# Layer 0's last grouped head, reordered at its end, and sixteen modulation loads moved to GpSimd's queue

## The chip, the cores and the metric

One NeuronCore of a Trainium2 chip runs the whole kernel. It has five engines with a queue of instructions each: TensorE (PE in the profile, with its weight loads as PEld), VectorE (DVE), ScalarE (ACT), GpSimd (POOL) and SyncE (SP), which here only issues transfers (DMAs). The metric is the device time of one execution in microseconds (us); lower is better.

## The reference

Two layers of a diffusion backbone work on 512 latent and 256 context tokens of width 1024, all in float32.

```python
hx = _rmsnorm(x, norm_g) * (1.0 + scale_x) + shift_x        # the same for the context: hc
a_att = _na_latent(qa, ka, va, cka, cva, rpb, rows)          # 8 heads, neighbourhood window plus all context keys
b_att = _gqa_latent(qb, k_all, v_all)                        # 8 query heads, 2 key heads, all 768 keys
o_a = (a_att * jax.nn.silu(a_z)) @ w_o_a
o_b = (b_att * jax.nn.silu(b_z)) @ w_o_b
merged = jax.nn.sigmoid(g_a) * o_a + jax.nn.sigmoid(g_b) * o_b
x_new = x + gate_x * (merged @ w_out)
```

`shift`, `scale` and `gate` are the modulation: `silu(c) @ w_ada + b_ada`, a vector times a 1024x3072 matrix for each layer, once for the latent and once for the context condition. In layer 0 the context tokens go through the same steps, except that they attend only to context keys (`c_a_att`, `c_b_att`). Layer 1 updates the latent tokens alone.

## The kernel before

**Precision.** Every matrix product of activations and weights is three matmuls on high and low parts (`mm3`, lines 352 to 354): high x high, high x low, low x high. So each operand has to be split: ScalarE copies the high part (`S.copy`, which rounds), and VectorE or GpSimd subtracts it from the source for the low part. Weights are split so in `load_w` (lines 322 and 325) and `load_w2` (337 and 339), where even tiles' low parts go to GpSimd and odd ones' to VectorE (`mix_lo`).

**Stages of a layer.** The projections come first, then neighbourhood attention by head, the grouped projections, grouped attention by head, and a merge: the branch's output projections (`o_chunks`, "a" as filler during grouped attention, "b" after it), and the output projection `w_out` with the residual. While a head's softmax runs, PE gets pieces of projections from a list, `fill`.

**A grouped head.** `gq_scores` (line 948) makes four score tiles of 768 columns in a score bank (`s`, two buffers of 1024 columns) and their softmax; `ctx_scores` (725) makes the context queries' scores. `gq_values` (964) transposes the probabilities in six steps of four blocks (670), splits them (673 on ACT, 674 on DVE) and multiplies by the values (973, 974) into the one value bank (`v`). `ctx_values` (741) does the same for the context's 256 columns (747, 748), also in the `v` bank. Each ends in `head_out` (677): ACT copies one half of the result (682), DVE adds the other (683), and GpSimd multiplies it into the gate path `zb` (684), 64 rows by 512 or 256 columns. `values_of` (866) calls the main values first, then the context's.

**After the last head.** `zb` has four blocks f of 768 columns; head h writes block h // 2. `hilo` (555) splits a block: ACT the high part `gbh` (558), GpSimd the low part `gbl` (559). `early` (985) splits blocks 0 to 2 before head 7's values are traced, and line 1003 splits block 3 after them. Then `o_chunks("b", ...)` takes four chunks of 256 output channels; a chunk has four pieces, for two f each of (0, 512) and (512, 768) columns, and a piece sums over the four blocks of `zb`. Its results lie in the `f` bank and five `x` banks that take the place of the score and value banks (`open_ps(x=5)`, line 997).

**The modulation of layer 1** is computed in layer 0. `ada_steps` (239) loads tiles of 128x512 from `w_ada` (251, buffer `rawb`, two of them) and multiplies each twice by the broadcast condition `cb` in one VectorE instruction with a running sum (258). The first 16 tiles come early in layer 0; the second 16 (line 1031) run in the merge, some after each of the six token tiles of `w_out`. `make_hx` (291) then builds layer 1's normalised input from each token tile, with the row norm on GpSimd (286, 288); the latent tiles are also stored to DRAM (1047), from where layer 1's merge reads them back.

**What sets the order.** The kernel is traced in program order, and a planner with a model of each instruction's cost lays every engine's queue out from it: among the instructions that are ready by its clock, it takes the earliest traced. A few chains are tied to program order by hand (`behind`, line 381, for the dot products on VectorE). Each queue then runs strictly in that order on the chip, so an instruction that waits holds everything behind it.

Of the kernel before, what the change touches and what calls it, by code (L numbers as in the profile page):

```python
# [12 lines left out]
ALU = mybir.AluOpType  # L13
# [55 lines left out]
def hybrid_kernel(es: ExitStack, tc, x, ctx, cvec, w_ada, w_ada0, small, gvec, w_in, w_o_a, w_o_b, w_out,  # L69
# [168 lines left out]

    def ada_steps(l, tiles, halves, nv, pool):

        cb = {}

        def load(h):
            cb[h] = pool.tile([128, 2, 512], F32, tag="cb", name=nm("cb"), bufs=1)
            for v in range(nv):
                src = cd[8 * v + 4 * h:8 * v + 4 * h + 4].rearrange("k p -> (k p)").unsqueeze(0)
                nc.sync.dma_start(cb[h][:, v, :], src.to_broadcast([128, 512]))

        def load_tile(h, i):
            cb["w"] = pool.tile([128, 512], F32, tag="rawb", name=nm("rawb"), bufs=2)  # L250
            nc.sync.dma_start(cb["w"], w_ada[l, h, i])

        def dot(h, i, v):
            if v == 0:
                load_tile(h, i)
            w = cb["w"]
            o = w if v == nv - 1 else pool.tile([128, 512], BF16, tag="junk", name=nm("junk"), bufs=1)
            behind(ON_DVE, lambda: V.tensor_tensor_reduce(o, w, cb[h][:, v, :], 1.0, 0.0, ALU.mult, ALU.add,
                                                          asum[:, i, h, v:v + 1]))
# [231 lines left out]
    def layer(l, hx, nxt, mid):  # L491
# [62 lines left out]

        def hilo(src, dst, fs):
            sv = src.rearrange("p (f n) -> p f n", f=4)
            for f in fs:
                S.copy(R(dst[0][:, f, :ntok]), sv[:, f, :ntok])
                G.tensor_tensor(R(dst[1][:, f, :ntok]), sv[:, f, :ntok], dst[0][:, f, :ntok], ALU.subtract)

# [3 lines left out]
        def o_chunks(br, prepare, evac):  # L564

            src = (w_o_a if br == "a" else w_o_b)[l]
            act = lambda part, k: gated[br][part][:, k, :]
            res = []
            for i in range(4):
                st = {}  # L570

                def ld(i=i, st=st):
                    st["w"] = load_w2(src, 256 * i, 4, mix_lo)
                pieces = [lambda f=f, n0=n0, n1=n1, i=i, st=st:
                          chan_proj(st["w"], f, act, n0, n1, lambda f, a, b, ps: evac(2 * i + f, a, b, ps))
                          for f in range(2) for n0, n1 in spans]
                res.append((ld, ([prepare] if i == 0 and prepare else []) + pieces))
            return res
# [72 lines left out]
        if True:  # L651
# [25 lines left out]
            def head_out(po, e, dst):  # L677
# [5 lines left out]
                V.tensor_tensor(t1[m:m + 64, :n], po[m:m + 64, :n], t1[m:m + 64, :n], ALU.add)  # L683
                G.tensor_tensor(dst, dst, t1[m:m + 64, :n], ALU.mult)

# [55 lines left out]
            def ctx_values(p, vsl, dst, e):  # L741
                hi, lo = transpose_split(
                    [(p[:, 256 * i + 128 * k:256 * i + 128 * k + 128], 256 * k + 128 * i)
                     for k in range(2) for i in range(2)])
                po = psw(256, "v")
                for k in range(2):
# [91 lines left out]
            def pipeline(fill, spread, scores_of, values_of, last=None, bg=[]):  # L838
# [10 lines left out]
                if last is not None:  # L849
                    run(fill, len(fill))  # L850
                    last()
                run(bg, len(bg))
                values_of(7, prev)
                run(fill, len(fill))

            akt = [k_tile(e, True) for e in range(2)]

            def na_first(h):
# [89 lines left out]
            def gq_scores(q, kh, kl):  # L948
# [13 lines left out]
                return ps_  # L962

            def gq_values(h, ps_):
                e, kv = h % 2, h // 4

                def vsl(t):
                    return R(vb[:, t, kv, 64 * e:64 * e + 128])
                po = psw(512, "v")
# [15 lines left out]
            def early():  # L985
# [7 lines left out]
            pipeline(fill, 8, gq_first, values_of(zb, gq_values), early, bg)  # L993
            gq_es.close()

        with tc.tile_pool(name=f"mrg{l}", bufs=1, reuse_waits="tile") as mp:
# [250 lines left out]
```

## Time and profile before

| what | value |
|---|---|
| runs (three) | 1145.15, 1145.70, 1145.71 us; median 1145.7 |
| the profiled execution | 1144.91 us, of which the span from first to last instruction is 1143.1 |
| PE busy | 1120.7 us, 98% |
| DVE, ACT, POOL busy | 816.3, 581.4, 480.6 us |
| transfers | SP's queue 133.87 MB of 135.08 MB; none issued by GpSimd |
| `rawb` loads | 64 of 256 KB, median 2.8 us from issue to landing |

The page of the profile gives busy time by engine over the span, the windows give the same by stretch, and the timeline lists each instruction with the idle time ahead of it on its engine and what ended that. PE is the engine whose idle time counts. Matmuls are pipelined and their shown durations overlap, so the pitch from one start to the next says more than the duration. A name such as `psx` or `gbl` is a buffer's name in the program.

### The profile page before, as it was taken

Reading aid. Unit: us, or ns where it says so; the run is one execution under the profiler, and the core shown is the slowest. Engines: PE = TensorE matmul, PEld = TensorE weight load, DVE = VectorE, ACT = ScalarE, POOL = GpSimd, SP = SyncE. Lnnn points to the kernel's source line nnn. Section 1 sums busy time; section 2 is a strip of 40 time slices with the busy share of each in tenths; the row PEclk is TensorE's granted clock in tenths of the full one; section 3 lists DMA queues with packets and bytes.
Section 4 is the critical chain, followed back from the end, with each engine's and each line's share of the span. In section 5 each row is a group of like instructions: output and inputs, shape, how many; then the busy total and the mean of one; then the engine's idle time right before and its main releaser. Section 6 shows DMA issues by size and latency. Waiting matters only on the chain.

```text
span 1143.1 us, 17425 instructions
## 1 busy us (share of the span) xinstructions
PE 1120.7 (98%) x6128; PEld 947.6 (83%) x6128; DVE 816.3 (71%) x1535; ACT 581.4 (51%) x1185; POOL 480.6 (42%) x449
## 2 busy tenths in 40 slices
PE   7999999999999999999999999999999999999998
PEld 5788888888988888888788787888887888887787
DVE  6777688887554786697588655469777665898573
ACT  6553366665443565666330355337666355766521
POOL 1073354553364333453511226345453664465311
PEclk9999999999999999999999999999999999999999
DMA  9645212333323232451434424633332333152133
GB/s 368 241 123 157 85 56 70 99 116 97 118 94 97 96 101 86 98 217 38 152 124 134 148 69 122 186 103 116 99 114 65 111 103 102 65 175 92 64 126 97
DMA packets 91886, 135.08 MB, mean 118 GB/s; under 512 B 10804, under 2 KB 55064, under 8 KB 91160
## 3 DMA queue, kind: packets, MB, share of 16 engines
q1 hardware_dynamic: 91520, 133.87, 36.9%
q8 instruction: 48, 0.79, 0.3%
q14 instruction: 38, 0.31, 0.1%
q10 hardware_dynamic: 280, 0.12, 0.0%
HBM read 116.63 MB, written 17.32 MB: 117 GB/s over the span
## 4 chain that ended last, share of the span: by engine, by line
PE 87%; DVE 5%; DMA 2%; ACT 2%; issue 2%; POOL 1%; SPq 0%; ACTq 0%; POOLq 0%; DVEq 0%
PE psx L352 12%; PE psx L354 12%; PE psx L353 12%; PE psf L352 10%; PE psf L353 10%; PE psf L354 10%; PE pst L670 5%; PE pss L792 3%; PE pss L719 2%; PE pss L720 2%; PE psv L974 2%; PE psv L973 1%; PE pst L432 1%; DVE ptl L674 1%; DMA rawb<-in_w_ada_dram 1%
## 5 line engine op out<-in xcount | busy, mean ns | idle before, releaser
L674 DVE TENSOR_TENSOR ptl<-pst,pth 128x512 fp32r<-128x512 f32 (+1 forms) x176 | 115.9, 671 | 43.4 <-ACT pth L673 42.4
L673 ACT CAST pth<-pst 128x512 fp32r<-128x512 f32 (+1 forms) x176 | 99.2, 577 | 93.2 <-PE pst L670 53.1
L352 PE MATMUL psf<-hx,whi 128*128 128x512 f32 (+1 forms) x368 | 140.1, 381 | 0.1
L339 POOL TENSOR_TENSOR wlo<-raw,whi 128x512 fp32r<-128x512 f32 x68 | 95.9, 1414 | 103.5 <-ACT whi L337 86.2
L353 PE MATMUL psf<-hx,whi 128*128 128x512 f32 (+1 forms) x368 | 138.0, 375 | 0.0
L354 PE MATMUL psf<-hx,wlo 128*128 128x512 f32 (+1 forms) x368 | 137.6, 374 | 0.0
L352 PE MATMUL psx<-whi,hx 128*128 128x512 f32 (+1 forms) x368 | 137.6, 375 | 0.0
L354 PE MATMUL psx<-whi,hx 128*128 128x512 f32 (+1 forms) x368 | 135.8, 369 | 0.0
L353 PE MATMUL psx<-wlo,hx 128*128 128x512 f32 (+1 forms) x368 | 135.7, 369 | 0.0
L337 ACT CAST whi<-raw 128x512 fp32r<-128x512 f32 x136 | 82.8, 620 | 51.3 <-DMA raw<-in_w_in_dram 32.5
L322 ACT CAST whi<-raw 128x512 fp32r<-128x512 f32 x88 | 53.9, 622 | 100.5 <-PE psx L354 38.3
L670 PE MATMUL pst<-ident,p 128*128 128x128 f32 x640 | 99.5, 272 | 1.4 <-DVE ptl L674 0.9
L325 POOL TENSOR_TENSOR wlo<-raw,whi 128x512 fp32r<-128x512 f32 x36 | 49.5, 1378 | 119.6 <-ACT whi L322 106.2
L339 DVE TENSOR_TENSOR wlo<-raw,whi 128x512 fp32r<-128x512 f32 x68 | 68.0, 1001 | 32.1 <-ACT whi L337 31.6
L670 PEld LDWEIGHTS pst<-ident,p 128*128 128x128 f32 x640 | 77.8, 141 | 13.4 <-DVE ptl L674 1.3
L660 POOL TENSOR_TENSOR p<-p,r 128x512 f32<-128x512 f32 (+1 forms) x64 | 83.5, 1305 | 4.9
L659 POOL TENSOR_SCALAR r<-r 128x1 f32<-128x1 f32 x64 | 22.2, 347 | 150.4 <-DVE r L654 126.9
L352 PEld LDWEIGHTS psx<-whi,hx 128*128 128x128 f32 x368 | 69.5, 189 | 12.3 <-issue 0.8
L354 PEld LDWEIGHTS psx<-whi,hx 128*128 128x128 f32 x368 | 69.4, 189 | 11.9
L354 PEld LDWEIGHTS psf<-hx,wlo 128*128 128x128 f32 x368 | 69.3, 188 | 11.7
L353 PEld LDWEIGHTS psx<-wlo,hx 128*128 128x128 f32 x368 | 69.5, 189 | 10.7
L352 PEld LDWEIGHTS psf<-hx,whi 128*128 128x128 f32 x368 | 69.4, 189 | 10.5 <-ACT zt L517 0.3
(253 smaller groups left out, 3049.7 us busy)
## 6 DMA issues: line engine op xcount, KB each, us to landing
raw<-in_w_in_dram SPq DMA_DIRECT2D x168, 256.0 KB, 2.9
rawb<-in_w_ada_dram SPq DMA_DIRECT2D x64, 256.0 KB, 2.8
gs<-zt SPq DMA_DIRECT2D x32, 256.0 KB, 2.0
raw<-in_w_out_dram SPq DMA_DIRECT2D x32, 256.0 KB, 2.9
tg<-gs SPq DMA_DIRECT2D x4, 1536.0 KB, 6.8
rawx<-in_w_ada_dram SPq DMA_DIRECT2D x8, 512.0 KB, 7.7
raw<-in_w_o_a_dram SPq DMA_DIRECT2D x16, 256.0 KB, 2.7
raw<-in_w_o_b_dram SPq DMA_DIRECT2D x16, 256.0 KB, 3.3
```

The source lines that it names most:

```text
L322: S.copy(hi[:, :n], raw[:, :n])
L325: e.tensor_tensor(lo[:, :n], raw[:, :n], F(hi[:, :n]), ALU.subtract)
L337: S.copy(hi, raw)
L339: lo_eng(i).tensor_tensor(lo, raw, F(hi), ALU.subtract)
L352: T.matmul(ps, lhs[0], rhs[0], start=first, stop=False)
L353: T.matmul(ps, lhs[0], rhs[1], start=False, stop=False)
L354: T.matmul(ps, lhs[1], rhs[0], start=False, stop=last)
L660: G.tensor_tensor(p[:, c0:c1], p[:, c0:c1], r[:, i:i + 1].to_broadcast([128, c1 - c0]), ALU.mult)
L670: T.transpose(pt[:, c0:c0 + 128], src, ident)
L673: S.copy(hi[:, n0:n1], pt[:, n0:n1])
L674: V.tensor_tensor(lo[:, n0:n1], pt[:, n0:n1], F(hi[:, n0:n1]), ALU.subtract)
L792: T.matmul(pss.rearrange("p (a b n) -> p a b n", a=2, b=2), qi, blocks_of(k, *at), start=b, stop=not b)
```

## The change

Six edits, of which all but the last two act on layer 0's head 7 alone:

1. In `pipeline`, `att["end"]` is set ahead of the last head's values. `values_of` then runs `ctx_values` first and the main values second, and `ctx_values` takes a score bank in place of the value bank.
2. `head_out` of that head, for both parts, multiplies on VectorE in place of GpSimd.
3. `early` makes block 2's low part on VectorE; blocks 0 and 1 stay on GpSimd.
4. Block 3 is split in two parts, columns 0 to 512 and 512 to 768, with the low parts on VectorE; and the first chunk of the "b" projection orders its pieces with the context columns first.
5. The second sixteen `rawb` loads are issued by GpSimd in place of SP. The two `cb` loads ahead of them stay with SP.
6. The four stores of the latent tiles to DRAM are issued by GpSimd in place of SP.

`ordered` and its two arguments `hi_after` and `lo_after` are defined and not used; neither is `att["turn"]`. For layer 1, with `first` false and one span, the generated work is as before.

```diff
-    def ada_steps(l, tiles, halves, nv, pool):
+    def ada_steps(l, tiles, halves, nv, pool, q=nc.sync):
...
-            nc.sync.dma_start(cb["w"], w_ada[l, h, i])
+            q.dma_start(cb["w"], w_ada[l, h, i])
...
-        def hilo(src, dst, fs):
+        def hilo(src, dst, fs, parts=None, lo=lambda f: G, hi_after=None, lo_after=None):
             sv = src.rearrange("p (f n) -> p f n", f=4)
+            ins = nc.cur_bb.bb.instructions
             for f in fs:
-                S.copy(R(dst[0][:, f, :ntok]), sv[:, f, :ntok])
-                G.tensor_tensor(R(dst[1][:, f, :ntok]), sv[:, f, :ntok], dst[0][:, f, :ntok], ALU.subtract)
+                for a, b in parts or [(0, ntok)]:
+                    S.copy(R(dst[0][:, f, a:b]), sv[:, f, a:b])
...
+                    lo(f).tensor_tensor(R(dst[1][:, f, a:b]), sv[:, f, a:b], dst[0][:, f, a:b], ALU.subtract)
...
-                pieces = [lambda f=f, n0=n0, n1=n1, i=i, st=st:
+                at = [(f, n) for f in range(2) for n in spans]
+                if br == "b" and i == 0:
+                    at.sort(key=lambda x: -x[1][0])
+                pieces = [lambda f=f, n0=n[0], n1=n[1], i=i, st=st:
                           chan_proj(st["w"], f, act, n0, n1, lambda f, a, b, ps: evac(2 * i + f, a, b, ps))
-                          for f in range(2) for n0, n1 in spans]
+                          for f, n in at]
...
-                G.tensor_tensor(dst, dst, t1[m:m + 64, :n], ALU.mult)
+                (V if (att["end"] and first) else G).tensor_tensor(dst, dst, t1[m:m + 64, :n], ALU.mult)
...
-                po = psw(256, "v")
+                po = psw(256, "s" if att["end"] else "v")
...
                 run(bg, len(bg))
+                att["end"] = last is not None
                 values_of(7, prev)
...
-            def values_of(dst, f):
+            def values_of(dst, f, ctx_vsl=None):
                 def g(h, st):
+                    if first and att["end"]:
+                        e = h % 2
+                        zv = dst.rearrange("p (f n) -> p f n", f=4)
+                        ctx_values(st[1], ctx_vsl(h), zv[64 * e:64 * e + 64, h // 2, 512:768], e)
                     vsl = f(h, st[0])
-                    if first:
+                    if first and not att["end"]:
...
-                hilo(zb, gated["b"], range(3))
+                hilo(zb, gated["b"], range(3), lo=lambda f: V if first and f == 2 else G)
...
-            hilo(zb, gated["b"], [3])
+            hilo(zb, gated["b"], [3], spans, lambda f: V if first else G)
...
-            bg = ada_steps(1, range(16), (1,), 2, mp) + [lambda: ada_mod(1)] if first else []
+            bg = ada_steps(1, range(16), (1,), 2, mp, G) + [lambda: ada_mod(1)] if first else []
...
-                            nc.sync.dma_start(xs1[128 * t:128 * t + 128, :], xt)
+                            G.dma_start(xs1[128 * t:128 * t + 128, :], xt)
```

More of the change, by code (lines that the diff above doesn't have):

```diff
@@ L553, in hilo_tiles, with ordered @@
             return [big(name + part).rearrange("p (f n) -> p f n", f=4) for part in "hl"]
-        def hilo(src, dst, fs):
+        def ordered(i, last):
+            tc.add_manual_dep(i, last, mybir.DependencyInfo(
+                mybir.DependencyClass.NoSync, mybir.DependencyReason.DATA), reason="program order")
+        def hilo(src, dst, fs, parts=None, lo=lambda f: G, hi_after=None, lo_after=None):
             sv = src.rearrange("p (f n) -> p f n", f=4)
+            ins = nc.cur_bb.bb.instructions
             for f in fs:
-                S.copy(R(dst[0][:, f, :ntok]), sv[:, f, :ntok])
-                G.tensor_tensor(R(dst[1][:, f, :ntok]), sv[:, f, :ntok], dst[0][:, f, :ntok], ALU.subtract)
+                for a, b in parts or [(0, ntok)]:
+                    S.copy(R(dst[0][:, f, a:b]), sv[:, f, a:b])
+                    if hi_after is not None and f > 0:
+                        ordered(ins[-1], hi_after)
+                    lo(f).tensor_tensor(R(dst[1][:, f, a:b]), sv[:, f, a:b], dst[0][:, f, a:b], ALU.subtract)
+                    if lo_after is not None and lo(f) is G:
+                        ordered(ins[-1], lo_after)
         def load_tg(c):
@@ L856, in layer @@
             akt = [k_tile(e, True) for e in range(2)]
+            att["end"], att["turn"] = False, 0
             def na_first(h):
@@ L962, in gq_scores, with gq_vsl @@
                 return ps_
+            def gq_vsl(h):
+                return lambda t: R(vb[:, t, h // 4, 64 * (h % 2):64 * (h % 2) + 128])
             def gq_values(h, ps_):
-                e, kv = h % 2, h // 4
-                def vsl(t):
-                    return R(vb[:, t, kv, 64 * e:64 * e + 128])
+                e = h % 2
+                vsl = gq_vsl(h)
                 po = psw(512, "v")
@@ L990, in early @@
                 gated["b"] = hilo_tiles("gb")
-                hilo(zb, gated["b"], range(3))
+                hilo(zb, gated["b"], range(3), lo=lambda f: V if first and f == 2 else G)
             bg = gate_steps((1,), att["p"]) if first else []
-            pipeline(fill, 8, gq_first, values_of(zb, gq_values), early, bg)
+            pipeline(fill, 8, gq_first, values_of(zb, gq_values, gq_vsl), early, bg)
             gq_es.close()
```

## The prediction

> **What bounds the kernel now.** I read the page's shares first, then the chain, then the windows.
>
> ```profile
> span 1143.1 us, 17425 instructions
> PE 1120.7 (98%) x6128; PEld 947.6 (83%) x6128; DVE 816.3 (71%) x1535; ACT 581.4 (51%) x1185; POOL 480.6 (42%) x449
> PE 87%; DVE 5%; DMA 2%; ACT 2%; issue 2%; POOL 1%; SPq 0%; ACTq 0%; POOLq 0%; DVEq 0%
> ```
>
> TensorE bounds the kernel: 1120.7 of 1143.1 us, so all its visible gaps together are 22.4 us. The change adds or removes no matmul, so it can win or lose only gaps. The windows (columns: width, then PE, PEld, DVE, ACT, POOL busy with instruction counts, granted clock, DMA share, GB/s) say where they are around the edits:
>
> ```profile
> 550.00:555.00 5.00, 5.00 (x32) 4.00 (x31) 4.08 (x6) 2.42 (x4) 4.18 (x3) 1.00 0.10 29
> 555.00:560.00 5.00, 3.23 (x20) 2.44 (x18) 1.65 (x3) 1.53 (x3) 4.23 (x3) 1.00 0.27 91
> 560.00:565.00 5.00, 4.78 (x26) 4.18 (x27) 0.17 (x1) 1.46 (x2) 3.69 (x3) 1.00 0.96 288
> 565.00:590.00 25.00, 25.00 (x145) 22.00 (x144) 24.06 (x46) 9.81 (x19) 2.97 (x3) 1.00 0.61 214
> 600.00:640.00 40.00, 39.43 (x173) 31.87 (x172) 33.03 (x82) 4.97 (x8) 5.53 (x4) 1.00 0.48 145
> 640.00:690.00 50.00, 50.00 (x247) 41.89 (x246) 28.35 (x44) 28.23 (x68) 11.08 (x16) 1.00 0.30 100
> 720.00:1143.00 423.00, 413.26 (x2120) 344.20 (x2118) 301.51 (x522) 218.64 (x430) 194.43 (x178) 1.00 0.34 107
> ```
>
> The end of layer 0's last grouped head is 550 to 565: PE idles 1.77 + 0.22 = 1.99 us there, then is full until the output projection, where 0.57 us is idle in 600 to 640. The clock is 1.00 throughout. That 0.57 is one wait in the table of waits (total, times, longest):
>
> ```profile
> PE psx L352 <- ACT whi L322: 0.6, 1, 0.6
> ```
>
> The timeline shows how the first two arise (start, length, then in brackets the idle time ahead of it and what ended it):
>
> ```profile
> 550.82 5.87 POOL L559 TENSOR_TENSOR gbl<-zb,gbh 128x768 fp32r<-128x768 f32 x3 [3.60 <-PE psf L353]
> 551.40 0.60 PE L670 MATMUL pst<-ident,p 128*128 128x128 f32 x4
> 551.76 0.48 PE L974 MATMUL psv<-ptl,vb 128*128 128x512 f32 x1
> 552.43 0.48 PE L352 MATMUL psf<-gbh,whi 128*128 128x512 f32 x1
> 555.34 0.40 PE L354 MATMUL psf<-gbh,wlo 128*128 128x512 f32 x1
> 555.57 0.40 PE L352 MATMUL psf<-gbh,whi 128*128 128x512 f32 x1
> 555.68 0.58 ACT L682 COPY ho<-psv 64x512 f32<-64x512 f32 x1
> 556.41 0.69 DVE L683 TENSOR_TENSOR ho<-psv,ho 64x512 f32<-64x512 f32 x1
> 556.65 1.30 POOL L339 TENSOR_TENSOR wlo<-raw,whi 128x512 fp32r<-128x512 f32 x1
> 556.75 0.50 PE L353 MATMUL psf<-gbl,whi 128*128 128x512 f32 x1 [0.79 <-POOL gbl L559]
> 557.33 0.28 PE L747 MATMUL psv<-pth,vb 128*128 128x256 f32 x1
> 558.03 1.28 POOL L684 TENSOR_TENSOR zb<-zb,ho 64x512 f32<-64x512 f32 x1
> 558.74 0.28 PE L354 MATMUL psx<-gbh,wlo 128*128 128x256 f32 x1
> 559.34 0.36 ACT L682 COPY ho<-psv 64x256 f32<-64x256 f32 x1 [3.09 <-POOL zb L684]
> 559.74 0.43 DVE L683 TENSOR_TENSOR ho<-psv,ho 64x256 f32<-64x256 f32 x1 [2.64 <-ACT ho L682]
> 560.22 0.50 PE L352 MATMUL psx<-gbh,whi 128*128 128x512 f32 x1 [1.21 <-DVE ho L683]
> 560.25 0.73 POOL L684 TENSOR_TENSOR zb<-zb,ho 64x256 f32<-64x256 f32 x1 [0.94 <-DVE ho L683]
> 561.01 0.84 ACT L558 CAST gbh<-zb 128x768 fp32r<-128x768 f32 x1 [1.30 <-POOL zb L684]
> 561.92 1.85 POOL L559 TENSOR_TENSOR gbl<-zb,gbh 128x768 fp32r<-128x768 f32 x1 [0.95 <-ACT gbh L558]
> ```
>
> GpSimd is one queue for three low parts of the gate (5.87 us), a weight split (1.30), both closing products (1.28, 0.73) and the fourth low part. PE first waits for the third low part (0.79 us). Then the main values' product waits behind the queue, ACT's context copy waits for it (3.09 us), DVE waits for ACT, and PE waits for the DVE step at 559.74 (1.21 us), which I read as the value bank that the projection takes over. From the main values' copy (555.68) to the finished fourth low part (561.92 + 1.85 = 563.77) pass 8.1 us.
>
> Matmul durations overlap, so gaps understate the loss; the pitch of two 512-column matmuls is 555.57 - 555.34 = 0.23 us, half that for 256 columns. First stop: 556.75 - 555.57 - 0.23 = 0.95 us. Second: 560.22 - 558.74 - 0.12 = 1.36 us. A group of four transposes takes 551.76 - 551.40 = 0.36. From 552.43 to 555.57 PE starts ten 512-column matmuls and one such group, 2.3 + 0.36 of 3.14 us: another 0.5 lost in stretched pitches. In all about 2.8 us.
>
> **The change, part by part.**
>
> *Third low part on DVE.* POOL loses 5.87 / 3 = 1.96 us; DVE gains one 128x768 operation.
>
> ```profile
> 551.43 1.78 DVE L339 TENSOR_TENSOR wlo<-raw,whi 128x512 fp32r<-128x512 f32 x1
> 568.10 0.68 DVE L325 TENSOR_TENSOR wlo<-raw,whi 128x512 fp32r<-128x512 f32 x1
> ```
>
> The same 128x512 operation takes 0.68 us alone and 1.78 us under POOL's low parts. So the new one costs 0.68 x 1.5 = 1.0 us alone, and up to 2.7 us against POOL. I take 1.0 plus part of a wait, 1.5 us, and keep both ends. It can't start before 550.82, since the tile has readers until then.
>
> [...]
>
> *Closing products, fourth low part on DVE.* POOL sheds 1.28 + 0.73 + 1.85 = 3.86 us. DVE takes a 64x512 and a 64x256 product (0.69 and 0.43, as its sums at 556.41 and 559.74) and low parts of 512 and 256 columns (0.68, and 0.43 at that width): 2.2 us. With the 1.5 above, 3.7 us go on a DVE that idles 15 - 4.08 - 1.65 - 0.17 = 9.1 us in 550 to 565. Hidden there; with that cover gone, as in 565 to 590 where DVE is busy 24.06 of 25, it would cost its full length. The main chain becomes ACT copy 0.58, DVE sum 0.69, DVE product 0.69, ACT cast of 512 columns about 0.6 (0.84 for 768), DVE low part 0.68: 3.2 us in place of 8.1.
>
> *Context values first, in a score bank.* Nothing is added: the same transposes and four matmuls, earlier. They no longer wait for the main values' bank, nor the context copy for POOL's product. The main values now come last, some 0.8 us later (four matmuls at 0.12, a transpose group at 0.36). What is late next is their bank: it comes free 0.58 + 0.69 = 1.3 us after the last value matmul.
>
> *Context columns first.* Two pieces of 12 matmuls at 0.12 = 2.9 us of work whose fourth part is ready early; this covers the 1.3 us bank wait, and with the first nine matmuls of a main piece (9 x 0.23 = 2.1) the 3.2 us chain. If the planner spends these pieces before the values end, part of the cover is gone, at up to 1.3 us.
>
> Sum of the tail: first stop and stretched pitches 1.45, of which 1.3 goes; second stop 1.36, of which 1.2 goes: **-2.5 us**, bounds -2.8 (all) and -0.7 (1.1 of contention and half of the 1.3 us bank wait left).
>
> *Sixteen 256 KB loads and four stores to GpSimd's queue.* SP sheds the issues; POOL takes them.
>
> ```profile
> L251 SPq DMA_DIRECT2D rawb<-in_w_ada_dram x16: 327/328/646, 563.3 to 633.5; - x16
> DMA to landing us min/median/max: 2.5/2.6/9.4
> DVE junk L258 <- DMA rawb<-in_w_ada_dram: 5.5, 6, 1.6
> 624.27 0.61 DVE wlo L325
> 624.90 3.50 DMA raw<-in_w_out_dram
> 629.19 1.32 POOL wlo L325
> 630.53 3.48 DMA raw<-in_w_out_dram
> 634.78 0.51 PE psx L352
> ```
>
> These lie in 599 to 638. With two buffers, each load is issued when a dot product ends, lands 2.6 us later, and DVE already waits 5.5 us for them. The trace has no POOL-issued DMA. Its cost on POOL lies between 0.3 us, SP's shortest issue, and 1.3 us, POOL's 128x512 operation; twenty cost 6 to 26 us on a POOL busy 5.53 of 40 and 11.08 of 50 us: room, but a load that waits for a dot product blocks the weight splits (L325) and the row norms (L286, L288) queued behind it, and PE waits for the former through the chain above. Landing: between no later and 1.3 us later each. Against it stands a gain: SP no longer holds weight loads behind waiting modulation loads; at most the 0.57 us that PE waits here. I take 0 for both together, nearest the rows as they stand, and keep -0.6 to +6.5: ten loads, five rounds of two buffers, come before the split at 624.27, and 5 x 1.3 = 6.5. The stores wait for a row tile before its norm does and cost POOL an issue each, under a PE with no gap in 640 to 690.
>
> The profiled execution took 1144.91 us (1143.1 and 1.8 around). 1144.91 - 2.5 = 1142.4; the runs' median is 0.8 higher, so 1145.7 - 2.5 = **1143.2 us**.
>
> **The rivals.**
>
> 1. *The tail gives little*: the third low part holds DVE under POOL, the splits of the last values queue behind it, or the planner, which orders by readiness, doesn't run the context first. For it: the 1.78 us row. Against: DVE's 9.1 idle us. -0.7: 1145.0.
>
> [...]
>
> 3. *Slower: POOL's queue holds modulation loads and weight splits against each other.* Place: 599 to 638; price 1.3 us per round, 5 x 1.3 - 2.5 = +4.0, 1149.7. It decides from (2.5 + 2.3) / 5 = 1.0 us per round. For it: no slack at 634.78. Against: POOL is idle seven eighths of that stage.
>
> 4. *The planner lays out layer 1 otherwise*, 720 to 1143 holding 9.7 us of PE gaps: a third of those, 3 us, either way on top of the forecast: 1140.2 or 1146.2. For it: the planner orders every later instruction by times that these edits shift. Against: the edits touch nothing of layer 1.
>
> **How the numbers follow.** No change is what lies within 0.2%, 2.3 us, about what a measurement can tell here: 1143.4 to 1148.0. Forecast 0.46, its own range 1142.2 to 1143.8, about 0.32 of it below the bound; rival 1 0.15; rival 2 0.08; rival 3 0.19; rival 4 0.12, half each way. Faster 0.32 + 0.06 = 0.38; same 0.14 + 0.15 + 0.08 + 0.06 = 0.43; slower 0.19. The range goes down to rival 4's good end and up to where half of rival 3 is left out: 1140.2 to 1148.6.
>
> **What would show it.** Right: PE's gaps between 550 and 565 fall from 1.99 us to under 0.5; L559 on POOL runs twice in a row, not three times; the last L684 is a DVE row; the step from the last ho copy to the last low part is near 3.5 us. DVE idle before L258 stays near 5.5 us and PE's wait for whi at L322 under 0.6. [...]

## The result and the profile after

| | before | after |
|---|---|---|
| median of 20 runs each | 1145.26 us | 1147.03 us |
| range of the runs | 1144.62 to 1146.57 | 1145.03 to 1148.30 |
| profiled execution | 1144.91 us, span 1143.1 | 1146.77 us, span 1144.8 |

The ratio after to before is 1.0015, 95% interval 1.0009 to 1.0021: about 1.8 us more, where the prediction had 2.5 us less. Of all runs, here and below, only two of the 11 of kernel 6 were slow ones (1863.2 and 3958.9 us), and its time leaves them out.

The profile of after has one row to cut the time with. Two matmul groups stand in the same place of both programs, one ahead of the change's first effect and one behind the "b" projection: a group of four transposes near 533 us, and the first matmul of the output projection (`mh` as its input). Their rows in the timeline of PE (start, length), first before, then after:

```profile
533.18 0.60 PE L670 MATMUL pst<-ident,p 128*128 128x128 f32 x4
590.65 0.40 PE L352 MATMUL psx<-whi,mh 128*128 128x512 f32 x1
```

```profile
533.72 0.60 PE L683 MATMUL pst<-ident,p 128*128 128x128 f32 x4
593.26 0.40 PE L352 MATMUL psx<-whi,mh 128*128 128x512 f32 x1
```

The **tail** (from the one to the other) grew from 57.47 to 59.54 us, +2.07. What lies ahead of it is 0.54 longer, which arises in the first 55 us, ahead of anything that the change touches, and the **rest**, from the second row to the end of the span, fell from 552.45 to 551.54, -0.91. Together 0.54 + 2.07 - 0.91 = 1.70, the difference of the spans. Tail and rest are used for every kernel below.

The windows of after (columns as in the prediction) show the same:

```profile
550.00:555.00 5.00, 4.37 (x31) 3.66 (x29) 4.12 (x4) 3.30 (x6) 2.75 (x2) 1.00 0.00 2
555.00:560.00 5.00, 2.73 (x11) 2.13 (x12) 3.56 (x5) 0.56 (x1) 4.77 (x4) 0.84 0.26 59
560.00:565.00 5.00, 5.00 (x28) 4.62 (x27) 3.93 (x8) 1.28 (x4) 0.00 (x0) 0.82 0.96 290
...
720.00:1144.80 424.80, 415.16 (x2128) 345.77 (x2126) 300.34 (x523) 218.72 (x430) 194.32 (x179) 1.00 0.35 108
```

PE is idle 0.63 + 2.27 = 2.90 us in 550 to 565, where it was 1.99, and the granted clock there is 0.84 in 555 to 560 and 0.82 in 560 to 565, where it was 1.00. Past 720 the idle time is 9.64 us, where it was 9.74. The table of PE's waits of after names what ended the idle time:

```profile
PE psv L994 <- DVE ptl L687: 3.7, 4, 1.7
PE psf L352 <- DVE tg L606: 2.0, 3, 1.1
...
PE pst L304 <- DVE y L298: 0.3, 1, 0.3
```

Both stops of before, for `gbl` and for the `ho` sum, are gone, and so is the wait for `whi`; in their place PE waits 1.7 us for the low part of a split and 1.1 us for an evacuation, both from VectorE. The timelines of the engines show why (lines of after; ACT, DVE, POOL and PE are put together here):

```profile
553.23 0.59 ACT L686 CAST pth<-pst 128x512 fp32r<-128x512 f32 x1 [0.41 <-PE pst L683]
554.14 0.58 ACT L686 CAST pth<-pst 128x512 fp32r<-128x512 f32 x1 [0.32 <-PE pst L683]
552.25 2.60 POOL L567 TENSOR_TENSOR gbl<-zb,gbh 128x768 fp32r<-128x768 f32 x1 [4.36 <-PE psf L353]
554.81 2.00 POOL L567 TENSOR_TENSOR gbl<-zb,gbh 128x768 fp32r<-128x768 f32 x1
552.21 0.96 DVE L567 TENSOR_TENSOR gbl<-zb,gbh 128x768 fp32r<-128x768 f32 x1
553.08 2.05 DVE L567 TENSOR_TENSOR gbl<-zb,gbh 128x256 fp32r<-128x256 f32 x1
555.06 0.41 DVE L606 SCALAR_TENSOR_TENSOR tg<-tg,psf 128x256 f32<-128x256 f32 x1
555.39 1.97 DVE L339 TENSOR_TENSOR wlo<-raw,whi 128x512 fp32r<-128x512 f32 x1
557.28 1.28 DVE L687 TENSOR_TENSOR ptl<-pst,pth 128x512 fp32r<-128x512 f32 x2
555.52 0.39 PE L352 MATMUL psf<-gbh,whi 128*128 128x256 f32 x1 [1.15 <-DVE tg L606]
558.01 0.51 PE L994 MATMUL psv<-ptl,vb 128*128 128x512 f32 x1 [1.75 <-DVE ptl L687]
559.44 0.58 ACT L695 COPY ho<-psv 64x512 f32<-64x512 f32 x1 [4.72 <-PE psv L994]
563.28 0.69 DVE L567 TENSOR_TENSOR gbl<-zb,gbh 128x512 fp32r<-128x512 f32 x1
```

The last two high parts `pth` are ready at 553.8 and 554.7. Their low parts start at 557.28, because VectorE's queue has four instructions ahead of them: block 2's low part (0.96 us), that of block 3's 256 context columns (2.05), the evacuation PE waits for first (0.41), and a weight split (1.97). The second and the fourth each end shortly after a low part of GpSimd does (0.28 us after 554.85, 0.55 after 556.81). That GpSimd has two low parts in a row and not three is as predicted, and so is the order of the values.

And then the clock. Windows of 1 us of after (last but two column: granted clock):

```profile
554.00:555.00 1.00, 0.37 (x2) 0.06 (x1) 1.00 (x1) 0.58 (x1) 1.00 (x2) 1.00 0.00 0
555.00:556.00 1.00, 0.48 (x4) 0.48 (x4) 1.00 (x3) 0.00 (x0) 1.00 (x1) 1.00 0.00 0
556.00:557.00 1.00, 0.26 (x3) 0.06 (x1) 1.00 (x1) 0.00 (x0) 1.00 (x2) 1.00 0.00 0
557.00:558.00 1.00, 0.00 (x0) 0.00 (x0) 1.00 (x3) 0.00 (x0) 1.00 (x1) 1.00 0.00 0
558.00:559.00 1.00, 0.99 (x3) 0.69 (x4) 0.56 (x1) 0.00 (x0) 1.00 (x2) 0.69 0.43 113
559.00:560.00 1.00, 1.00 (x5) 0.90 (x5) 0.00 (x0) 0.56 (x1) 0.77 (x2) 0.50 0.87 184
560.00:561.00 1.00, 1.00 (x7) 1.00 (x6) 0.69 (x1) 0.02 (x1) 0.00 (x0) 0.50 0.84 297
561.00:562.00 1.00, 1.00 (x7) 1.00 (x7) 0.82 (x2) 0.00 (x0) 0.00 (x0) 0.61 1.01 311
```

Behind 4 us in which PE was busy 0.37 + 0.48 + 0.26 + 0.00 = 1.11 us, it runs at a granted clock of 0.50 for some 3.4 us (an estimate from these windows: two whole ones, 0.62 of the one ahead of them and 0.78 of the one behind, if 0.69 and 0.61 are means of 1.00 and 0.50; in windows of 0.1 us the clock is 0.50 from 558.4 to 561.7), and looks fully busy there (2.00 us of the 2 from 559 to 561): a gap count can't see this loss.

### The profile page after: what moved, and what is told of

Read it like the earlier page. It is cut to its first block, busy times and chain, and to the rows that moved or that the text cites. A ratio compares the mean times of both kernels' runs of the same rounds, so it can differ in the third digit from the quotient of the medians.

```text
span 1144.8 us, 17440 instructions
## 1 busy us (share of the span) xinstructions
PE 1122.5 (98%) x6128; PEld 951.0 (83%) x6128; DVE 818.6 (72%) x1540; ACT 582.1 (51%) x1186; POOL 486.6 (43%) x465
## 4 chain that ended last, share of the span: by engine, by line
PE 88%; DVE 5%; issue 2%; DMA 2%; ACT 2%; POOL 0%; ACTq 0%; POOLq 0%; DVEq 0%
PE psx L352 13%; PE psx L354 12%; PE psx L353 12%; PE psf L352 10%; PE psf L353 10%; PE psf L354 10%; PE pst L683 5%; PE pss L805 2%; PE pss L732 2%; PE pss L733 2%; PE psv L994 2%; PE psv L993 1%; PE pst L432 1%; DVE ptl L687 1%; DMA rawb<-in_w_ada_dram 1%
```

## The experiments

**Theory A**: the loss is in the tail, from low parts that VectorE's queue puts ahead of the last splits, and from the clock that drops behind the wait. **Rival B**: it comes from the modulation loads in GpSimd's queue. A third possibility is that the order of the values itself is bad. All times are medians; before was measured beside each group of kernels (1145.23, 1145.22, 1144.98 and 1145.20 us), and the ratios are against that. Line numbers in the diffs' kernels differ a little from those of after.

| kernel | time, us | ratio, 95% interval | tail, us | rest, us |
|---|---|---|---|---|
| before | 1145.26 | | 57.47 | 552.45 |
| after | 1147.03 | 1.0015 (1.0009 to 1.0021) | 59.54 | 551.54 |
| 1 tail only, loads on SP | 1147.54 | 1.0018 (1.0009 to 1.0027) | 59.65 | 552.2 |
| 2 loads and stores only | 1144.56 | 0.9991 (0.9983 to 1.0000) | 57.48 | 551.7 |
| 3 after, no low part on VectorE | 1142.79 | 0.9977 (0.9968 to 0.9987) | 55.93 | 550.9 |
| 4 after, low parts behind the splits | 1144.12 | 0.9989 (0.9980 to 0.9997) | 57.19 | 551.9 |
| 5 after, PE kept busy | 1147.42 | 1.0019 (1.0010 to 1.0028) | 58.19 | 554.1 |
| 6 kernel 3, loads on SP | 1144.02 | 0.9986 (0.9976 to 0.9995) | 55.91 | 552.5 |
| 7 after, block 2 back on GpSimd | 1143.32 | 0.9982 (0.9974 to 0.9991) | 56.19 | 551.3 |
| 8 all low parts on VectorE | 1144.73 | 0.9993 (0.9984 to 1.0001) | 57.24 | 552.0 |
| 9 kernel 1, PE kept busy | 1146.11 | 1.0010 (1.0001 to 1.0019) | 58.19 | 552.6 |
| 10 after, PE kept half busy | 1147.71 | 1.0024 (1.0014 to 1.0035) | 58.17 | 553.3 |
| 11 before, context first only | 1144.00 | 0.9991 (0.9982 to 1.0000) | 56.06 | 552.1 |
| 12 kernel 11, loads on GpSimd | 1143.73 | 0.9988 (0.9979 to 0.9997) | 56.06 | 551.7 |

Tail and rest are from one profiled execution each; where two kernels have the same tail in the program, the values agree within 0.11 us (59.54 and 59.65; 57.47 and 57.48; 55.93 and 55.91; 56.06 twice; 58.19 twice). By the times alone, the gains of kernels 2, 8 and 11 can't be told from no change: their intervals reach 1.0000 or 1.0001.

### 1 and 2: which half of the change costs

Kernel 1 is after without its last two edits:

```diff
-            bg = ada_steps(1, range(16), (1,), 2, mp, G) + ...
+            bg = ada_steps(1, range(16), (1,), 2, mp) + ...
-                            G.dma_start(xs1[128 * t:128 * t + 128, :], xt)
+                            nc.sync.dma_start(xs1[128 * t:128 * t + 128, :], xt)
```

> The change with its loads and stores back on SP's queue (edits 5 and 6 undone); the planned order of the tail is the same as in the changed kernel. Theory A (the loss is in the tail: VectorE takes two low parts and a weight split ahead of the last two splits of head 7's values, so TensorE stands still, and its clock then drops): slower than the changed kernel by 0.3 to 1.0 us, since the loads' move won something; 1.8 to 3 us above the kernel before; TensorE gaps of 2.5 to 3 us and a clock of 0.8 to 0.9 between 555 and 565. Theory B (the loss comes from GpSimd's queue holding loads and weight splits against each other): back to the kernel before, within 0.5 us.

Kernel 2 is before with these two edits alone (the same lines the other way round).

> The kernel before with only the sixteen loads and the four stores moved to GpSimd's queue (edits 5 and 6). Theory A: 0.3 to 0.9 us faster than before, since TensorE's 0.57 us wait for the output projection's weights near 634 goes; gaps in 550 to 565 stay near 2 us. Theory B: 1 to 2.5 us slower than before, with new TensorE waits near 620 to 650.

The tail alone has the whole loss, 1147.54; the loads alone come out at or below before, 1144.56. Rival B falls. The loads' own gain is in the rest (551.7 against 552.45) and leaves the tail alone.

### 3: no low part on VectorE

```diff
-                hilo(zb, gated["b"], range(3), lo=lambda f: V if first and f == 2 else G)
+                hilo(zb, gated["b"], range(3), lo=lambda f: G)
...
-            hilo(zb, gated["b"], [3], spans, lambda f: V if first else G)
+            hilo(zb, gated["b"], [3], spans, lambda f: G)
```

> The change with all four low parts of the gate on GpSimd again (edit 3 and the engine of edit 4 undone; context first, score bank, VectorE products and the loads' move stay). Theory A1 (the low parts in VectorE's queue are what delays the splits): TensorE's waits for ptl fall below 0.5 us, the clock stays at 1.00, and the wait for GpSimd's third low part (0.8 us) comes back; 0.5 to 2 us faster than the kernel before. [...]

1142.79: 4.2 us less than after, and less than before too. Windows of this kernel, in which PE idles 0.49 us in place of 2.90:

```profile
550.00:555.00 5.00, 4.51 (x35) 4.01 (x33) 4.31 (x6) 2.95 (x5) 3.11 (x2) 1.00 0.00 2
555.00:560.00 5.00, 5.00 (x24) 3.83 (x25) 2.08 (x3) 1.20 (x2) 5.00 (x4) 1.00 0.77 249
```

And its timelines of POOL and DVE:

```profile
551.89 7.03 POOL L567 TENSOR_TENSOR gbl<-zb,gbh 128x768 fp32r<-128x768 f32 x4 [4.35 <-PE psf L353]
...
552.49 1.78 DVE L339 TENSOR_TENSOR wlo<-raw,whi 128x512 fp32r<-128x512 f32 x1
554.20 1.27 DVE L687 TENSOR_TENSOR ptl<-pst,pth 128x512 fp32r<-128x512 f32 x2
```

The last splits start at 554.20, and what PE still waits is for them, behind the weight split. GpSimd works on four low parts in a row up to 558.9, and PE never waits for one: the stop for the third low part that before had (0.79 us) doesn't come back, against the expectation. In the new order PE has other matmuls at that point. The third possibility falls with it, since order and bank are those of after.

### 4: the low parts on VectorE, but behind the splits

Block 2's and block 3's low parts stay on VectorE and are tied behind the last split in its queue:

```diff
...
+                for f, a, b in ((2, 0, ntok), (3, 512, 768), (3, 0, 512)):
+                    hi, lo = [g[:, f, a:b] for g in gated["b"]]
+                    if f == 3:
+                        S.copy(R(hi), sv[:, f, a:b])
+                    V.tensor_tensor(R(lo), sv[:, f, a:b], hi, ALU.subtract)
+                    ordered(nc.cur_bb.bb.instructions[-1], att["ptl"])
...
```

> The change with VectorE's low parts of blocks 2 and 3 tied behind the last split of head 7's values, by order alone; engines as in the change. Theory A1: TensorE's waits for ptl and for the filler's bank (1.15 and 1.75 us) fall below 0.7 us together, the clock stays at 1.00, and the time is 1.5 to 3.5 us below the changed kernel's neighbour before, 1142 to 1144. Rival C (a leftover wait, for the value bank or for block 2's now later low part, takes their place): TensorE gaps of 1.5 us or more remain between 555 and 563, and the time is not below the kernel before by more than 0.7 us.

1144.12, just above the expected 1142 to 1144, and 1.1 us below before, where rival C had at most 0.7. The half clock is gone (the mean clock of the profiled execution is 1.000, against 0.999 in after) and the wait for the split is 0.5 us, but PE now waits for the low parts themselves (PE's waits in the tail of this kernel, the two parts take VectorE 2.79 us from 555.91):

```profile
PE psf L353 <- DVE gbl L1032: 1.0, 2, 0.8
PE psv L995 <- DVE ptl L687: 0.5, 1, 0.5
```

So order alone wins back 2.4 of the 3.6 us of tail between after and kernel 3, with the half clock in it (1.35 by the next experiment); the other 1.3 goes with low parts that now come late.

### 5, 9 and 10: what the clock costs by itself

Extra matmuls that nobody reads fill PE's idle time. They stand in the queue where PE would only wait, so the splits are as late as in after:

```diff
                     T.matmul(po, vsl(k), hi, start=k == 0, stop=False)
+                    if first and att["end"] and k == 4:
+                        d = psw(512, "s")
+                        for _ in range(12):
+                            T.matmul(d, vsl(k), hi, start=True, stop=True)
...
```

> The kernel after with 12 more 128x512 matmuls on TensorE, of the last head's fifth high part, into a bank of the scores that nobody reads; they stand behind the fifth group's first value matmul and ahead of the wait for its low part. At 0.23 us each they are 2.8 us of work and fit in the idle time from about 554.2 to 558.0. Nothing is left out. Theory A (two costs: the low parts that queue ahead of the last splits on VectorE, about 2.7 us of waiting, and on top the half clock that follows the wait, about 1.6 us): the waiting matmul still starts near 558.0, but the granted clock stays 1.00 behind it; the time falls by 1.6 us, from 1147.0 to 1145.4. Rival (the low clock costs nothing of its own, or comes from the start-up of the stage and not from the idle time): the time stays at 1147.0 or above, and the clock still reads about 0.5 from 558 to 562.

With 12 of them the clock stays at 1.00 (windows of this kernel), the last splits start as late as before (557.10), and the tail falls by 59.54 - 58.19 = 1.35 us. The half clock is a cost of its own, of that size here.

```profile
555.00:560.00 5.00, 4.51 (x27) 3.63 (x26) 3.79 (x5) 0.58 (x1) 4.59 (x4) 1.00 0.28 79
560.00:565.00 5.00, 5.00 (x29) 4.35 (x28) 3.84 (x9) 1.77 (x4) 0.00 (x0) 1.00 1.00 307
```

But the time is 1147.42 in place of the expected 1145.4: the rest of the profiled execution grew by 2.6 us. Two rows of this kernel's tables of waits belong to that:

```profile
PE pst L304 <- DVE y L298: 1.0, 1, 1.0
...
DVE junk L258 <- DMA rawb<-in_w_ada_dram: 8.1, 6, 2.0
```

PE waits 1.0 us for `y`, where it was 0.3, and VectorE waits 8.1 us for modulation loads, where after has 5.1. From the last splits to the end of the dot products, all engines run the same instructions in the same order in both profiles, by name and shape, and kernel 5 is 1.35 us ahead (counted from the transposes) up to one dot product, whose load took 3.8 us from issue to landing in place of 2.9. Its row in the timelines of after and of kernel 5:

```profile
611.01 0.69 DVE L258 CUSTOM_DVE_ANT_0 junk<-rawb,cb 128x512 bf16<-128x512 f32 x1 [0.51 <-DMA rawb<-in_w_ada_dram]
```

```profile
610.51 0.69 DVE L258 CUSTOM_DVE_ANT_0 junk<-rawb,cb 128x512 bf16<-128x512 f32 x1 [1.59 <-DMA rawb<-in_w_ada_dram]
```

There the lead falls to 0.27 us, and a second late load (3.9 us in place of 3.3) makes it 0.65 us of delay near 641. Was that the loads, or is a gain in the tail always given back? Kernel 9 has the same matmuls, with the loads and stores on SP (as kernel 1).

> The kernel of the tail alone (all edits but the loads and stores, which SP issues as before), with the 12 extra 128x512 matmuls ahead of the wait for the fifth group's low part. Nothing is left out. From the group of four transposes near 534 to the output projection's first matmul passed 59.65 us in the tail alone, and 58.19 with the matmuls and the loads on GpSimd. Theory A (the half clock costs 1.4 us there, and the projection gave it back in the first of these kernels because a modulation load that GpSimd issued landed late): 58.2 to 58.3 us again, and since SP issues the loads the end moves as well: 1147.5 - 1.4 = 1146.1. Rival (what the matmuls win is always given back, since VectorE's chain of dot products in the output projection doesn't start earlier): 1147.3 or above, with TensorE waiting for a weight split or for y near 635 to 650.

1146.11, 1.4 us less than kernel 1 (1.2 if each is taken against the before measured beside it), with a tail of 58.19 and a rest of 552.6, near kernel 1's. With SP issuing, what the tail wins reaches the end; with the loads on GpSimd's queue it didn't. Why the loads landed late in kernel 5 stays open. Kernel 10 has 6 matmuls in place of 12, loads on GpSimd.

> The kernel after with 6 of the extra matmuls in place of 12, 1.4 us of work, so that the idle time before the late low part is cut to about 1.5 us and not filled. Nothing is left out. If the half clock follows from a stretch of little work as long as the one of after (2.9 us of 4 idle): the clock stays 1.00, and the time to the output projection is as with 12, 58.2 us; the end at 1147 if the give-back is as with 12, at 1145.7 if that one was of its order of instructions alone. If it follows any wait of over a microsecond: the clock drops again, 59.5 us, 1147.

The tail is again 58.17 and the clock of the profiled execution 1.00, though PE waits 1.77 us in one piece (timeline of this kernel):

```profile
557.66 0.50 PE L999 MATMUL psv<-ptl,vb 128*128 128x512 f32 x1 [1.77 <-DVE ptl L687]
```

So 1.8 us without any matmul didn't drop it in this execution, and a wait of over a microsecond wasn't enough by itself there. Whether it dropped in other runs of this kernel the record doesn't show; the mean clock of four of its eight is 0.998. The end, 1147.71, didn't move either, and in this profile too VectorE waited longer for modulation loads (7.2 us) and PE for `y` (0.9).

### 7 and 8: which low part, and the queue or GpSimd's work beside it

Kernel 7 takes only block 2's low part off VectorE:

```diff
-                hilo(zb, gated["b"], range(3), lo=lambda f: V if first and f == 2 else G)
+                hilo(zb, gated["b"], range(3), lo=lambda f: G)
```

> The kernel after with the third block's low part back on GpSimd; the fourth block's parts (256 and 512 columns) and the products stay on VectorE. On VectorE the 256-column part alone stands ahead of the last two splits, in place of 2.93 us of two parts. Theory A: 0.4 to 0.8 us are left of that delay, so the last splits start at 554.6 to 555.0 and TensorE waits 0.5 to 1.2 us; no half clock; 1142.8 to 1143.6. If it is the fourth block's low parts that cost the time (the 512-column one is the last link of the chain): near 1147, as after.

1143.32, tail 56.19. Block 3's two parts on VectorE cost 56.19 - 55.93 = 0.26 us of tail; block 2's costs 59.54 - 56.19 = 3.35, of which 1.35 is the clock. Timelines of DVE and POOL of this kernel:

```profile
552.63 0.43 DVE L567 TENSOR_TENSOR gbl<-zb,gbh 128x256 fp32r<-128x256 f32 x1
552.68 2.08 POOL L567 TENSOR_TENSOR gbl<-zb,gbh 128x768 fp32r<-128x768 f32 x1 [4.36 <-PE psf L353]
...
555.23 1.28 DVE L687 TENSOR_TENSOR ptl<-pst,pth 128x512 fp32r<-128x512 f32 x2
```

The 256-column part starts here just ahead of GpSimd's first low part and takes 0.43 us. In after, block 2's part had that place, and the 256 columns, which came behind it, took 2.05.

Kernel 8 puts blocks 0 and 1 on VectorE as well, so that GpSimd does no low part there:

```diff
-                hilo(zb, gated["b"], range(3), lo=lambda f: V if first and f == 2 else G)
+                hilo(zb, gated["b"], range(3), lo=lambda f: V if first else G)
```

> [...] If the order in the queue is all (each part 1.0 us or less alone, three and a quarter of them 3.3 us): the last splits come at about 557, the time is 1146 to 1147.5, as after. [...]

Timelines of POOL and DVE of this kernel:

```profile
551.66 1.29 POOL L339 TENSOR_TENSOR wlo<-raw,whi 128x512 fp32r<-128x512 f32 x1 [4.29 <-ACT whi L337]
551.68 2.08 DVE L567 TENSOR_TENSOR gbl<-zb,gbh 128x768 fp32r<-128x768 f32 x1
...
554.55 0.41 DVE L606 SCALAR_TENSOR_TENSOR tg<-tg,psf 128x256 f32<-128x256 f32 x1
554.89 1.28 DVE L567 TENSOR_TENSOR gbl<-zb,gbh 128x768 fp32r<-128x768 f32 x2
556.09 0.68 DVE L339 TENSOR_TENSOR wlo<-raw,whi 128x512 fp32r<-128x512 f32 x1
556.69 1.27 DVE L687 TENSOR_TENSOR ptl<-pst,pth 128x512 fp32r<-128x512 f32 x2
```

The first part took 2.08 us, where the expectation had 1.0 or less for each: it began 0.02 us after a weight split on GpSimd, and ended 0.8 us after that one did. The later ones have no two-input operation of GpSimd beside them, and there the pair that after has (768 and 256 columns, 1.28 us together) and the weight split (0.68) take less than half of after's 2.05 + 0.96 and 1.97. With twice the parts in the queue the splits are as late as in after, 23.49 us behind the transposes and 23.56, as the order alone has it; but PE idles 1.84 us in 550 to 565 in place of 2.90, the mean clock of the profiled execution is 1.000, and the time, 1144.73, is below the 1146 that order alone was to give at least. So the order and the longer operations beside GpSimd's each had a part. At the lengths they have in kernel 8, after's four instructions would take about 1.28 + 0.41 + 0.68 = 2.4 us, where they took 557.28 - 552.21 = 5.07: by this estimate, about half of their delay is the greater length beside GpSimd's low parts.

### 6, 11 and 12: what the reordering gains

Kernel 6 is kernel 3 with SP's loads and stores back (1144.02).

> The kernel after with all the gate's low parts on GpSimd and the loads and stores issued by SP again: the context first, the score bank, the products on VectorE and nothing else. If the parts add (loads and stores -0.7 us as in the run of them alone, the tail -1.7): 1143.5, ratio 0.9985. If the loads on GpSimd only gained by cover that the tail gives too: 1142.8, as with them. If the two need each other: above 1144. TensorE's gaps between 550 and 565 near 0.5 us, the clock 1.00.

It came out at the edge of the expectation's third case, "if the two need each other". But the tails of kernels 3 and 6 are the same (55.93 and 55.91), so what differs lies in the rest, and no run shows why.

Kernel 11 is before with the first edit, block 3 in two parts and the order of columns alone; against kernel 6 it differs in one line:

```diff
-                (V if (att["end"] and first) else G).tensor_tensor(dst, dst, t1[m:m + 64, :n], ALU.mult)
+                G.tensor_tensor(dst, dst, t1[m:m + 64, :n], ALU.mult)
```

> The kernel before with the first two edits alone: context values first in a score bank, context columns first, the fourth low part in two parts. The products, all low parts and all loads and stores are where they were before. GpSimd then has four low parts (7.0 us from 552), a weight split (1.3), the main product (1.3), ScalarE's cast 0.6 and the 512-column low part (1.3), so that the last part ends at about 563.4, against 561.5 with the products on VectorE. If TensorE has enough other pieces there, as the run without low parts on VectorE suggests: 1144.1, the same as with the products on VectorE, and it is the order of the values that gains. If the products on VectorE are what shortens the end: up to 1.9 us more, 1146.0.

The same time, 1144.02 and 1144.00, and tails of 55.91 and 56.06. On GpSimd the last low part ends at 563.5 (timeline of kernel 11), and PE doesn't wait for it:

```profile
552.33 6.56 POOL L567 TENSOR_TENSOR gbl<-zb,gbh 128x768 fp32r<-128x768 f32 x4 [2.75 <-PE psf L354]
...
562.24 1.30 POOL L567 TENSOR_TENSOR gbl<-zb,gbh 128x512 fp32r<-128x512 f32 x1 [0.73 <-ACT gbh L564]
```

Kernel 12 is kernel 11 with the loads and stores on GpSimd (the diff of kernel 1, the other way round).

> The kernel before with the context values first in a score bank, the context columns first, and the loads and stores issued by GpSimd; no step of the head and no low part goes to VectorE. Nothing is left out. If the products on VectorE are worth nothing also where GpSimd issues loads: the time of the kernel without low parts on VectorE, 1142.8, ratio 0.9977 to 0.998. If GpSimd's queue (four low parts, a weight split, the main product, two loads of 0.67 us and then the last low part) makes that last part late: it ends at about 564.9, TensorE waits for it near 563 to 565, and the time is 1144 or above. TensorE's gaps from 550 to 565 near 0.5 us in the first case, the clock 1.00 in both.

1143.73, between the two cases; its tail is 56.06 again, so GpSimd's queue doesn't hold the last low part against PE. The interval overlaps kernel 3's. The loads' own worth can be read in five places, each time against the before measured beside the kernel: -0.7 us (kernel 2 less before), -1.2 (3 less 6), -0.5 (after less 1), -0.5 (12 less 11) and +1.1 (5 less 9). The interval of most kernels is 1 us either way, so none of the five is sure by itself; four of them gain, and their mean is -0.4. The best version is kernel 3, 0.9977 of before.

The tail now adds up from kernel to kernel: context first -1.41 (11), products on VectorE -0.15 (6), block 3's low part there +0.28 (7), block 2's +2.00 and the clock +1.35 (after): +2.07 in all. The two small steps are near the 0.11 us by which equal tails differ. Context values first and context columns first were not taken apart.

## Why the prediction was wrong

**The step that failed** is the term of the tail, in the sentence that "3.7 us go on a DVE that idles 15 - 4.08 - 1.65 - 0.17 = 9.1 us in 550 to 565. Hidden there". The sum of idle time is right, its place is wrong. Of the 15 us only those before the last splits matter, and in 550 to 555, quoted in the prediction itself, VectorE was busy 4.08 of 5. In after the first low part starts at 552.2, in the middle of it; the planner put it ahead of splits whose high parts were ready 1.6 and 2.5 us later, and the sum has no term for PE's wait for these. Measured from the transposes near 533, the last splits start 23.56 us later in after and 21.08 in kernel 7; of these 2.5 us PE lost 2.0, before the clock.

**The size that was wrong** isn't that of the third low part. 1.5 us were taken for it, and it took 0.96, near the 1.0 of the working; it started 0.04 us ahead of GpSimd's first low part. The time went into the next one: the 256 columns of the fourth block, put at 0.43 us, took 2.05. The weight split behind took 1.97, where 1.78 had been its row before. The bound of -0.7 has 1.1 us of contention for the third low part, a term that no run shows; in its place the runs show the two instructions behind it 1.62 us longer than in kernel 7 (2.05 - 0.43) and 1.29 longer than in kernel 8 (1.97 - 0.68). The two splits that PE waited for, which read `pst` from PSUM, weren't longer: the pair takes 1.27 us in kernel 3, beside GpSimd's low parts, and 1.27 in kernel 8 without them.

**The clock** was no term at all. "The clock is 1.00 throughout" was a reading of before; the half clock cost 1.35 us of tail in after (kernel 5, and 1.46 by kernel 9).

**The two stops of before.** Both went, as forecast, and by the edits that order the work: 1.41 us of tail by kernel 11. The 2.5 us of gain were too many: PE's idle time in 550 to 565 falls from 1.99 to 0.56 us in kernel 11, as much as the tail, so the 0.5 us of "stretched pitches" and the pitch corrections of the stops brought nothing that the tail shows; and the wait of 0.5 us for the last splits behind the weight split, in kernels 3, 6, 7, 11 and 12, was not seen. The third low part on VectorE was costed against the first stop, but the reordering had already removed that stop (kernel 3).

**The main chain** from the last `ho` copy to the last low part was to be 3.2 us; it is 559.44 to 563.97, 4.5, with an evacuation between the sum and the product on VectorE. It was covered, and would have been with the product on GpSimd too (kernel 11): nothing depended on the length that was computed.

**The loads** were put at 0, and gain in four pairs of kernels of five, 0.4 us in the mean. GpSimd's issue takes 0.54 us in the median, inside 0.3 to 1.3. GpSimd's issues (the 14 behind the first two), by tile, in after:

```profile
L251 POOL DMA_DIRECT2D rawb<-in_w_ada_dram x14: 536/537/558, 603.6 to 640.6; - x14
```

The transfers of after by queue (last column: median us from issue to landing):

```profile
rawb<-in_w_ada_dram POOLq DMA_DIRECT2D x16, 256.0 KB, 3.0
```

3.0 us against the 2.6 of the same loads before. The 0.08 of rival 2 stands for a price that no run shows; what the runs show is that VectorE waits 5.1 us for these loads in after, 5.5 before, and the rest got 0.91 us shorter.

**The rivals.** The first had the right mechanism ("the third low part holds DVE under POOL, the splits of the last values queue behind it") and the wrong sign: it was priced at a smaller gain, since its bound counted no wait of PE for the queue behind the part. In after that is a wait of PE for `ptl` up to 558.0 (1.75 us). Rival 3 named the right side for another place; between 599 and 638 nothing was lost in after. Rival 4 falls: 9.64 us of gaps past 720 against 9.74.

**What was luck.** 1147.03 lies inside the range of 1140.2 to 1148.6 and inside what the prediction called no change, but no case in it led there: rival 1 was a smaller gain, and rival 4 had layer 1 laid out otherwise. The width of the range covered a loss that was not foreseen.

## What to carry to other kernels

Work is hidden by idle time ahead of the next instruction that the bounding engine waits for, not by the sum of idle time in a stage; so read a narrow window around each consumer, and the queue behind the new instruction. When a wait of the matrix engine grows, price the clock after it as well (1.35 us of tail here), and remember that a busy count didn't show the halved clock (2.00 us of 2 at 0.50); a mark at the same instruction in both traces did. Parts of a change that win by themselves (the order here) are worth timing apart from those added to support them.

## What the runs showed of the hardware

**The granted clock fell in after, where PE's longest wait was 1.75 us.** 4 us with 1.11 us of work, this wait in them, were followed by some 3.4 us at 0.50; 256-column matmuls then start 0.21 us apart (559.20 to 561.55 in 11 steps), where it was 0.12 (551.41 to 552.01 in 5 steps). In before, 2.0 us of gaps within 4.3 us (555.96 to 560.22) left it at 1.00. How much idle time is enough, and what sets the length of the stretch at 0.50, no run here shows. The mean clock also differs from run to run of the same kernel:

| mean clock of the run | after: runs, their mean time | kernel 3 | kernel 5 |
|---|---|---|---|
| 1.000 | 1, 1145.0 us | 6 | 9 |
| 0.999 | 8, 1146.7 us | 4 | 2 |
| 0.998 | 5, 1147.1 us | 0 | 0 |
| 0.996 | 6, 1147.8 us | 0 | 0 |

Kernel 10, whose profiled execution kept 1.00 in the tail, has 0.998 in 4 of its 8 runs and 0.999 in the others. So the slower runs of after (1145.0 to 1148.3) tend to be those with the lower clock. It isn't the only source of spread: kernel 5 goes from 1145.3 to 1148.8 at 0.999 and 1.000.

**Where subtractions on VectorE and GpSimd overlapped, one or both took longer, in all of these rows but the last.** All but the last have both inputs in SBUF. In after, block 2's part on VectorE started 0.04 us ahead of GpSimd's first and took 0.96 us; GpSimd's took 2.60, against 1.85 in before with VectorE idle (the row at 561.92). The 256 columns started under that part, took 2.05 (0.43 in kernel 7, where they started 0.05 us ahead of a part on GpSimd, which took 2.08) and ended 0.28 us after it. The weight split started under GpSimd's second part, took 1.97 (0.68 in kernel 8, with no such operation of GpSimd beside it) and ended 0.55 us after it. In kernel 8, GpSimd's weight split started 0.02 us ahead and took 1.29, the part on VectorE took 2.08 and ended 0.8 us after it. The last two splits, with `pst` from PSUM, took 1.27 us together in kernel 3, beside GpSimd's low parts, and in kernel 8 without them. Whether the place of the operands or the order of the starts makes the difference, no run here shows: none varies one of them alone.
